# Weight sums of an up product made in device memory by adding transfers, and twelve of its tiles instead of eight in seven products

## The chip, the cores and the metric

The kernel runs on one core of one Trainium2 chip. The metric is device time in microseconds (us) of one run, and the number told is the median of several runs. Engines: PE (TensorE), DVE (VectorE), ACT (ScalarE), POOL (GpSimd), and SP (SyncE), which here only issues transfers.

## The reference

One layer of an encoder trunk on x of 1 x 512 x 1024, all in float32:

```
h  = rmsnorm(x, g_pre_mix)
q, k, v, g, u, sv, a_ret, a_sgu = split(h @ w_in)
y_ret = retention(q, k, v, g) @ w_ret_o           # 4 heads, chunks of 128
y_sgu = (gelu(u) * spatial(layernorm(gelu(sv)))) @ w_sgu_o
x1 = x + rmsnorm((sigmoid(a_ret) * y_ret + sigmoid(a_sgu) * y_sgu) @ w_out, g_post_mix)
h2 = rmsnorm(x1, g_pre_ffn)
a, b = split(conv3(h2 @ w_up))                    # 1024 -> 2 x 2816
y  = x1 + rmsnorm((gelu(a) * b) @ w_down, g_post_ffn)
```

The change is about `h2 @ w_up`.

## The kernel before, in words

**Precision.** Every matrix is split in a high and a low part (fp32r). ACT writes the high part (`copy`, L100), DVE subtracts it from the source to get the low part (`split`, L119), and PE makes three matmuls for each product of blocks: high by high, high by low, low by high.

**Weights.** All weights lie in one array `wall` in device memory, in blocks of 128 x 1024 (512 KB). A list of units gives the order in which they are used. `w_get` hands out a unit and loads ahead of it. A unit of the kind `blk` (`w_block`, L172) is a whole block: SP loads it into one of four `raw` buffers (L176), and its two parts go into two of nine slots. The four `raw` buffers are shared by all weights until the end.

**Seven products.** A pair of weight blocks against a pair of activation halves can be multiplied as a 2 x 2 matrix of blocks in seven products instead of eight (class `Pair`: `part1`, `part2`, `part3`; each product is 12 matmuls of 128 x 256, L926). That needs sums of the four weight quarters: T1 = B11 + B12, T3 = B12 + B22 (signs folded into the stored weights), T2 = T1 + B22, T4 = T2 + B21. `w_form` (L194) loads the two blocks (L198, L199), makes the sums in `raw` (L205, L206, L208, L211) and splits each of the seven forms, 512 columns wide, into one slot. In the gate stage POOL makes T2 and T4, in the up stage DVE makes all four. The matching sums of the activations (S1 to S4, `h2_forms`) are made once.

**The up product.** It has 22 tiles; tile i is 128 gate columns and 128 linear columns, in blocks UP0+2i and UP0+2i+1. Tiles 0 to 3, 20 and 21 are made whole: two `f_block` of 24 matmuls of 128 x 512 each (L300 to L302). Tiles 4 to 19 are taken as eight couples (`COUPLES`): the first tile by `Pair`, the second whole, its two `f_block` standing between the parts of the first. After each couple `tile_done` makes the convolution (L1247, L1250, L1254), gelu and product for both tiles. At some tiles `down_forms` makes sums of the results for the down product, whose low parts are partly made by adding transfers of POOL (`split_added`, L1273).

**What sets the order.** The program is recorded, and a scheduler then orders the instructions of each engine; `issue_after` ties an instruction behind another one, `keep_in_program_order` keeps those that carry it in the order of the program. On each engine's queue the order is then fixed: a transfer that an engine issues stands in its queue between its other instructions. Retention (heads 0 to 3, states `st`, keys `kz`, scores `sm`, decay `dec`, outputs normed with `rs`, `orstd`, `oshift`) and the SGU's `sv` product (L755, seven products too, with weights `sb` and `raw` that POOL adds to by L265 and L271) run up to about 200 us, the u, gate and mixing stages to 400, the output product and norms to 470, the up product to 669, the down product to 763.

Of the kernel before, what the change touches and what calls it, by code (L numbers as in the profile page):

```python
# [10 lines left out]
F32 = mybir.dt.float32  # L11
# [4 lines left out]
P = 128  # L16
D = 1024
S = 512
# [34 lines left out]
def tile_block(ctx: ExitStack, tc, xT, x, wall, par, cs, wsp, bsp, gpost, gffn, out):  # L53
# [30 lines left out]
    def tmp(n="tmp", shape=(P, S)):  # L84
        return sb.tile(list(shape), F32, tag="tmp", bufs=6, name=nm(n))
# [10 lines left out]
    def const(n, shape):  # L96
        return sb.tile(list(shape), F32, tag=n, bufs=1, name=n)

    def copy(o, i):
        return nc.scalar.activation(out=o, in_=i, func=AF.Copy)  # L100

    def two(t):
        return t.rearrange("p (n c) -> p n c", n=2)
# [24 lines left out]
    while i < NW:  # L128
        pair = [(f, i) for f in FORMS]
        if i == SV0:  # L130
            units += [(f, k) for f in ("s11", "sT1", "sT2") for k in range(2)]
            units += [(f, k) for k in range(2) for f in ("s22", "sT3")]
            units += [(f, k) for f in ("s21", "sT4") for k in range(2)]
            i = U0
        elif i == U0:
            us, gs = ([[(f, k + n * m) for f in FORMS] for n in range(KD // 2)] for k, m in ((U0, 2), (GATE0, 4)))
            ws = [("blk", GATE0 + 4 * (n // 2) + 2 + n % 2) for n in range(KD)]
            for what, n in MIDDLE:
                units += {"W": lambda: ws[n : n + 1], "U1": lambda: us[n][:4], "U2": lambda: us[n][4:],
                          "G1": lambda: gs[n][:4], "G2": lambda: gs[n][4:]}.get(what, list)()  # L140
            i = GATE0 + 2 * KD
        elif GATE0 <= i < GATE1:
            units += pair[:4] + [("blk", i + 2)] + pair[4:] + [("blk", i + 3)]
            i += 4
        elif i == UP0 + 2 * COUPLES[0][0]:
            for a, b in COUPLES:
                pair = [(f, UP0 + 2 * a) for f in FORMS]
                units += pair[:4] + [("blk", UP0 + 2 * b)] + pair[4:] + [("blk", UP0 + 2 * b + 1)]
            i = UP0 + 2 * COUPLES[-1][1] + 2
# [44 lines left out]
    def w_form(form, i):  # L194
# [19 lines left out]
        split(hi, lo, w_raw[form])  # L214
        return hi, lo

    def w_down(form, i):

        if form == "q":
            raw = w_raw["q"] = raw_tile()  # L220
            nc.sync.dma_start(raw, wall[i])
            raw = raw[:, : 3 * 256]
        else:
            b, raw = w_raw["q"], raw_tile()
            two = "p (n c) -> p n c"
# [50 lines left out]
        return hi, lo  # L276

    def w_unit(u):
        return w_block(u[1]) if u[0] == "blk" else (w_down if u[0] in "qt" else w_sv if u[0][0] == "s" else w_form)(*u)

    def w_size(u):
        return 2 if u[0] in ("blk", "q", "t") or u[0][0] == "s" else 1

    def w_get(look=LOOK):

# [623 lines left out]
    class Pair:  # L909
# [3 lines left out]
        def __init__(self, func, alloc, a=None, scale=None):  # L913
            self.func, self.t, self.scale = func, [alloc(), alloc()], scale
            self.h, self.l, self.forms = a or (xh, xl, forms)
            self.b = [ps() for _ in range(3)]
            self.two = in_turn if a is None else two

        def product(self, b, act, first, w=None):
            wh, wl = w or w_get()  # L920
            o = self.b[b][:, T0]
            for k in range(4):
                c = slice(k * P, (k + 1) * P)
                h_, l_ = act(k)
                for n, (w_, a_) in enumerate(((wh, h_), (wh, l_), (wl, h_))):
                    self.last = nc.tensor.matmul(  # L926
                        o, w_[:, c], a_, start=first and k == n == 0, stop=k == 3 and n == 2,
                        skip_group_check=True,
                    )
            pe_last[0] = self.last.ins  # L930
            return self.two(o)
# [27 lines left out]
        def part2(self):  # L959
            c0, c1 = self.t  # L960
            o = self.product(0, self.s("S3"), False)
            copy(two(c1[:, T1]), o)
            v.tensor_sub(two(c1[:, T1]), self.two(self.b[2][:, T0]), two(c1[:, T1]))
            self.w = w_get(), w_get()

        def part3(self):
            c0, c1 = self.t
# [340 lines left out]

    def tile_done(i, o):
        gated(*(conv(t, 2 * i + s_) for s_, t in enumerate(o)))  # L1310
        if i < COUPLES[-1][1]:
            if i in (7, 9, 11, 13, 17):
                down_forms(len(dforms))
        elif len(dforms) < EAGER:
            down_forms(len(dforms))

    def h2_forms(k):
# [9 lines left out]
            split(h_, l_, s_)  # L1327
            h2forms[n] += [(h_[:, t], l_[:, t]) for t in (T0, T1)]

    couples = dict(COUPLES)  # L1330
    i = 0
    while i < NF:
        if i in couples:
            p = Pair(None, lambda: tmp("c"), (h2h, h2l, h2forms))
            p.part1()
            o = [f_block(h2h, h2l, KD)]
            p.part2()
            o.append(f_block(h2h, h2l, KD, p.part3))
            tile_done(i, p.t)
            tile_done(i + 1, o)  # L1340
            i += 2
        else:
            o = []
            for e in (2 * i, 2 * i + 1):
                o.append(early_o[e] if e < EARLY else f_block(h2h, h2l, KD))
            tile_done(i, o)
            for k in {0: (0,), 1: (2,)}.get(i, ()):
                h2_forms(k)
            i += 1
# [234 lines left out]
    ], 1)  # L1584


def _up(a):

    for i, _ in COUPLES:
        b, c = a[2 * i].reshape(P, 2, S), a[2 * i + 1].reshape(P, 2, S)  # L1590
        a[2 * i : 2 * i + 2] = np.stack([
            np.concatenate([b[:, 0], c[:, 0]], -1), np.concatenate([c[:, 1], b[:, 1]], -1),
        ])
    return a
# [84 lines left out]
```

## Time and profile before

| | |
|---|---|
| runs | 782.95, 783.85, 784.19 us; median 783.85 |
| the profiled execution: span from first to last instruction | 782.6 us |
| median of the runs less that span | 1.25 us |
| instructions | 13472 |
| busy: PE, DVE, ACT, POOL | 774.5, 639.5, 485.2, 103.5 us |
| granted clock of TensorE | 0.997 |
| moved by transfers | 104.80 MB, mean 134 GB/s |

Times in the views are microseconds from the span's start. A group's row gives line, engine, operation, out<-in with shapes and count, then busy us and mean ns of one, then the engine's idle time ahead of it with its releasers. PE's matmuls overlap, so that the distance between two starts, not the duration of one, is what a matmul costs. The page names lines of the kernel before; in the changed kernel the same lines stand lower (`copy` at L105, the issue of the plain copies at L127, of the adding transfers at L119, the adding loads L265 and L271 at L319 and L325, `rsqrt` L459 and L462 at L515 and L518, `shift` L723 at L779).

### The profile page before, as it was taken

What the parts mean: (1) busy time and instruction counts of PE and PEld (TensorE: products, weight loads), DVE (VectorE), ACT (ScalarE), POOL (GpSimd) and SP (SyncE); (2) the same over time, 40 slices, a digit from 0 to 9 for tenths busy, and PEclk for the clock granted to TensorE, in tenths of its full rate; (3) what the DMA queues carried; (4) which work ended last, traced back from release to release, by engine and by line L of the source; (5) the groups of instructions that cost most, each with busy time, mean ns of one, the idle gap of its engine ahead of it and who ended that gap; (6) DMA issues with size and microseconds to landing.
All of it is one profiled execution on the core that took longest, in us unless ns stands there. A gap on an engine that the chain in (4) does not pass through costs nothing.

```text
span 782.6 us, 13472 instructions
## 1 busy us (share of the span) xinstructions
PE 774.5 (99%) x5139; PEld 720.7 (92%) x5139; DVE 639.5 (82%) x1093; ACT 485.2 (62%) x878; POOL 103.5 (13%) x132
## 2 busy tenths in 40 slices
PE   9999999999999999999999999999999999999996
PEld 8888998998999999999998998999999998999996
DVE  6567987789789988877765679989999889886987
ACT  7555568688466766644454686657777568644542
POOL 0040001130021102033211200001111012200001
PEclk9999999999999999999999999999999999999998
DMA  8783224453223233233459120435555375733344
GB/s 288 271 246 102 81 82 162 108 122 108 81 91 126 82 122 121 83 110 106 138 171 337 54 81 28 124 107 141 142 148 149 108 199 111 171 114 107 109 162 162
DMA packets 35889, 104.80 MB, mean 134 GB/s; under 512 B 4400, under 2 KB 6320, under 8 KB 35824
## 3 DMA queue, kind: packets, MB, share of 16 engines
q1 hardware_dynamic: 27936, 87.81, 34.0%
q0 software_dynamic: 7024, 14.95, 9.0%
q10 hardware_dynamic: 864, 1.18, 0.4%
q8 instruction: 40, 0.66, 0.4%
q14 instruction: 25, 0.20, 0.1%
HBM read 91.34 MB, written 4.19 MB: 122 GB/s over the span
## 4 chain that ended last, share of the span: by engine, by line
PE 92%; DVE 3%; DMA 3%; issue 1%; ACT 0%; POOLq 0%; DVEq 0%; POOL 0%; ACTq 0%
PE ps L926 24%; PE ps L300 12%; PE ps L302 12%; PE ps L301 12%; PE ps L1372 7%; PE ps L755 5%; PE ps L634 4%; PE ps L636 4%; PE ps L635 4%; DMA raw<-wall 3%; PE ps L1109 2%; PE ps L1108 2%; PE ps L1107 2%; DVE dl L119 1%; PE ps L997 1%
## 5 line engine op out<-in xcount | busy, mean ns | idle before, releaser
L119 DVE TENSOR_TENSOR wl<-raw,wh 128x1024 fp32r<-128x1024 f32 (+1 forms) x84 | 96.0, 1152 | 54.3 <-issue 19.1
L100 ACT ACTIVATE wf<-raw 128x512 fp32r<-128x512 f32 x140 | 85.6, 625 | 67.3 <-PE ps L301 19.4
L926 PE MATMUL ps<-sh,wf 128*128 128x256 f32 x640 | 117.4, 276 | 0.1
L119 DVE TENSOR_TENSOR wf<-raw,wf 128x512 fp32r<-128x512 f32 x140 | 107.0, 774 | 9.2 <-ACT wf L100 8.6
L926 PEld LDWEIGHTS ps<-sh,wf 128*128 128x128 f32 x640 | 101.9, 192 | 1.1 <-ACT sig L100 0.5
L100 ACT ACTIVATE wh<-raw 128x1024 fp32r<-128x1024 f32 (+2 forms) x88 | 84.8, 977 | 28.5 <-DMA raw<-wall 14.0
L300 PE MATMUL ps<-h2h,wh 128*128 128x512 f32 (+1 forms) x256 | 90.6, 354 | 0.0
L301 PE MATMUL ps<-h2l,wh 128*128 128x512 f32 (+1 forms) x256 | 90.4, 353 | 0.0
L302 PE MATMUL ps<-h2h,wl 128*128 128x512 f32 (+1 forms) x256 | 90.4, 353 | 0.0
L926 PE MATMUL ps<-sl,wf 128*128 128x256 f32 x320 | 88.0, 275 | 0.0
L926 PEld LDWEIGHTS ps<-sl,wf 128*128 128x128 f32 x320 | 61.4, 192 | 0.4
L1372 PE MATMUL ps<-dh,fh 128*128 128x256 f32 x216 | 59.6, 276 | 0.3 <-DVE yy L1409 0.3
L1372 PE MATMUL ps<-dl,fh 128*128 128x256 f32 x216 | 59.5, 275 | 0.0
L1372 PE MATMUL ps<-dh,fl 128*128 128x256 f32 x216 | 59.4, 275 | 0.0
L100 ACT ACTIVATE dh<-raw 128x768 fp32r<-128x768 f32 (+1 forms) x36 | 33.6, 950 | 33.8 <-DVE raw L231 15.2
L302 PEld LDWEIGHTS ps<-h2h,wl 128*128 128x128 f32 x256 | 48.6, 190 | 5.1
L301 PEld LDWEIGHTS ps<-h2l,wh 128*128 128x128 f32 x256 | 48.6, 190 | 4.5
L300 PEld LDWEIGHTS ps<-h2h,wh 128*128 128x128 f32 x256 | 48.6, 190 | 4.5
L926 PE MATMUL ps<-xh,wf 128*128 128x256 f32 x288 | 52.2, 275 | 0.0
L636 PE MATMUL ps<-wh,xl 128*128 128x512 f32 x128 | 48.5, 379 | 0.0
L635 PE MATMUL ps<-wl,xh 128*128 128x512 f32 x128 | 48.5, 379 | 0.0
L634 PE MATMUL ps<-wh,xh 128*128 128x512 f32 x128 | 48.5, 380 | 0.0
(343 smaller groups left out, 2171.6 us busy)
## 6 DMA issues: line engine op xcount, KB each, us to landing
raw<-wall SPq DMA_DIRECT2D x144, 512.0 KB, 3.7
x<-x SPq DMA_DIRECT2D x24, 256.0 KB, 6.0
fl<-gp POOLq DMA_DIRECT2D x12, 256.0 KB, 3.8
swap<-qkraw POOLq DMA_DIRECT2D x16, 128.0 KB, 4.8
x<-x POOLq DMA_DIRECT2D x8, 256.0 KB, 2.3
fl<-fs POOLq DMA_DIRECT2D x8, 256.0 KB, 4.3
xT<-xT SPq DMA_DIRECT2D x7, 256.0 KB, 5.0
xT<-xT POOLq DMA_DIRECT2D x4, 256.0 KB, 4.1
```

The lines of the kernel that those rows point to most:

```text
L100: return nc.scalar.activation(out=o, in_=i, func=AF.Copy)
L119: low[0] = nc.vector.tensor_sub(lo, src, as32(hi)).ins
L300: nc.tensor.matmul(o, ah, bh, start=start, stop=False, skip_group_check=skip)
L301: nc.tensor.matmul(o, ah, bl, start=False, stop=False, skip_group_check=skip)
L302: pe_last[0] = nc.tensor.matmul(o, al, bh, start=False, stop=stop, skip_group_check=skip).ins
L634: nc.tensor.matmul(acc[t], xh[k][:, c], turns(wh[:, f]), start=k == 0, stop=False)
L635: nc.tensor.matmul(acc[t], xh[k][:, c], turns(wl[:, f]), start=False, stop=False)
L636: part_end[0] = nc.tensor.matmul(acc[t], xl[k][:, c], turns(wh[:, f]), start=False, stop=k == KD - 1)
L755: nc.tensor.matmul(bank[t], a_[:, c], turns(w_[:, f]), start=first and k == i == 0, stop=last and k == 3 and i == 2, skip_group_check=True,)
L926: self.last = nc.tensor.matmul(o, w_[:, c], a_, start=first and k == n == 0, stop=k == 3 and n == 2, skip_group_check=True,)
L1107: nc.tensor.matmul(o, ah, turns(bh), start=k == 0, stop=False)
L1372: nc.tensor.matmul(o, a_[:, c], turns(w_[:, f]), start=j == t == i == 0, stop=j == DP - 1 and i == 2 and n not in (M2, M3, M4), skip_group ...
```

## The change

Tiles 4 to 19 become four groups of four (`GROUPS`). In each, the first three tiles a, b and c go through `Pair` and the fourth is whole, so that twelve of the 16 tiles are made in seven products rather than eight. The weight sums of these twelve tiles are made in device memory: `sum{i}_0` holds T1 and T2 side by side (512 KB), `sum{i}_1` T3 and `sum{i}_2` T4 (256 KB each). They are made during the earlier stages, at every 17th call of `copy` from the 36th on. Step n of 15 issues, on ACT right behind that copy, three plain transfers that fill tile n's sums, and on POOL four adding transfers: two for tile n-1, one for n-2, one for n-3. In all 36 issues on ACT and 48 on POOL. Counted in program order, these copies start at 75.6, 104.2, 134.1, 159.2, 169.9, 187.9, 211.8, 229.3, 249.7, 268.4, 288.5, 308.9, 329.4, 354.4 and 375.9 us in the profile of before.

In the up stage the forms are loaded and split 1024 wide, two forms at once (`u1` the block itself, `u2` T1 and T2, `u4` T4 and a quarter, two loads into one buffer), and T3 (`u3`) 512 wide. DVE's 32 sums of the up stage are gone. The rearranging of these weights on the host (`_up`) is gone too. `down_forms` are made at the same tiles as before.

```diff
-COUPLES = [(i, i + 1) for i in range(4, 20, 2)]
+GROUPS = range(4, 20, 4)
+SEVENS = [i + n for i in GROUPS for n in range(3)]
+SUMS_FROM, SUMS_EVERY = 36, 17
+FORMS_AT = (7, 9, 11, 13, 17, 19, 20, 21)
...
     def copy(o, i):
-        return nc.scalar.activation(out=o, in_=i, func=AF.Copy)
+        done = nc.scalar.activation(out=o, in_=i, func=AF.Copy)
+        copies[0] += 1
+        n, r = divmod(copies[0] - SUMS_FROM, SUMS_EVERY)
+        if n >= 0 == r:
+            sums_step(n, done.ins)
+        return done
...
+    def sums_step(n, after):
+
+        def add(o, i):
+            tc.keep_in_program_order(nc.gpsimd.dma_start(o, i, accum_op=ALU.add))
+
+        for m in range(n, n - 4, -1):
+            if 0 <= m < len(SEVENS):
+                (t12, t3, t4), i = sums[m], UP0 + 2 * SEVENS[m]
+                if m == n:
+                    with tc.issue_after(after):
+                        for o, src in ((t12, wall[i + 1]), (t3, wall[i + 1, :, :S]), (t4, wall[i, :, S:])):
+                            nc.scalar.dma_start(o, src)
+                elif m == n - 1:
+                    add(t12[:, :S], wall[i, :, :S])
+                    add(t3, wall[i + 1, :, S:])
+                elif m == n - 2:
+                    add(t12[:, S:], t12[:, :S])
+                else:
+                    add(t4, t12[:, S:])
...
+            for g in GROUPS:
+                a, b, c = ([(f, g + n) for f in ("u1", "u2", "u3", "u4")] for n in range(3))
+                w = [("blk", UP0 + 2 * (g + 3) + n) for n in range(2)]
+                units += a[:2] + b[:2] + a[2:3] + w[:1] + a[3:] + b[2:3] + c[:2] + b[3:] + c[2:3] + w[1:] + c[3:]
...
+    def w_up(form, i):
+
+        t12, t3, t4 = sums[SEVENS.index(i)]
+        raw, i = raw_tile(), UP0 + 2 * i
+        if form == "u3":
+            raw = raw[:, :S]
+            nc.sync.dma_start(raw, t3)
+            w = slot("wf", 0, 1088)
+            lo, hi = w[:, AT_64 : AT_64 + S], w[:, S + AT_192 : 2 * S + AT_192]
+        else:
+            if form == "u4":
+                nc.sync.dma_start(raw[:, :S], t4)
+                nc.sync.dma_start(raw[:, S:], wall[i + 1, :, S:])
+            else:
+                nc.sync.dma_start(raw, wall[i] if form == "u1" else t12)
+            hi, lo = slot("wf", AT_192), slot("wf", AT_64)
+        split(hi, lo, raw)
+        return hi, lo
...
+        if i in GROUPS:
+            a, b = seven(), seven(blk)
+            a.part2()
             o = [f_block(h2h, h2l, KD)]
-            p.part2()
-            o.append(f_block(h2h, h2l, KD, p.part3))
-            tile_done(i, p.t)
-            tile_done(i + 1, o)
-            i += 2
+            a.part3()
+            tile_done(i, a.t)
+            b.part2()
+            c = seven()
+            b.part3()
+            tile_done(i + 1, b.t)
+            c.part2()
+            o.append(f_block(h2h, h2l, KD, c.part3))
+            tile_done(i + 2, c.t)
+            tile_done(i + 3, o)
+            i += 4
```

Three places of the new order. First POOL near the third and fourth head's norms, before (`raw` and `sb` are adding loads for the `sv` product, `xT` a load of x):

```order
L856 DMA xT_329_1674<-xT 128x512
L856 DMA xT_331_1678<-xT 128x512
L459 TENSOR_SCALAR rs_318_1590<-mv_770 128x4
L462 TENSOR_TENSOR orstd_771<-rs_318_1590,nhalf_440 128x4
L723 TENSOR_TENSOR oshift_772<-oshift_772,orstd_771 128x4
```

And the same place of POOL in the changed kernel (`sum5_0` is the first sum tile of tile 5, and so on):

```order
L912 DMA xT_329_1724<-xT 128x512
L912 DMA xT_331_1728<-xT 128x512
L119 DMA sum6_0_69<-wall 128x512
L119 DMA sum6_1_70<-wall 128x512
L119 DMA sum5_0_66<-sum5_0_66 128x512
L119 DMA sum4_2_65<-sum4_0_63 128x512
L319 DMA raw_370_1883<-wall 128x1024
L515 TENSOR_SCALAR rs_318_1640<-mv_806 128x4
L518 TENSOR_TENSOR orstd_807<-rs_318_1640,nhalf_476 128x4
L779 TENSOR_TENSOR oshift_808<-oshift_808,orstd_807 128x4
```

Four adding transfers of the sums came in, and the first adding load of `raw` stands ahead of `rs`, `orstd` and `oshift`; before it stood right behind them.

Second ACT from the last head's `kz` to its `dec`, before (`sh` are high parts for the `sv` product):

```order
L100 ACTIVATE kz_1702<-kt_1700 128x512
L566 ACT_TABLE_LOAD
L566 ACTIVATE dec_1706<-near_503 128x128
L100 ACTIVATE sh_1687<-xs_1682 128x512
L566 ACTIVATE dec_1706<-near_503 128x128
L555 ACTIVATE dec_1706<-dd_501,lg 128x128
```

And in the changed kernel:

```order
L105 ACTIVATE kz_1752<-kt_1750 128x512
L127 DMA sum_0_72<-wall 16x8192
L105 ACTIVATE sh_1737<-xs_1732 128x512
L127 DMA sum_1_73<-wall 128x512
L105 ACTIVATE sh_1741<-xg_1726 128x512
L127 DMA sum_2_74<-wall 128x512
L622 ACT_TABLE_LOAD
L622 ACTIVATE dec_1763<-near_539 128x128 x2
L611 ACTIVATE dec_1763<-dd_537,lg 128x128 x2
```

The fourth step's three plain transfers stand between `kz` and `dec`, and a second `sh` moved ahead of `dec`.

Third SP's loads at the start of the up product's first group, in the changed kernel; before, each couple had two loads for its pair (L198, L199) and two for its whole tile (L176):

```order
L266 DMA raw_937_5458<-wall 128x1024
L266 DMA raw_941_5489<-sum4_0_63 128x1024
L266 DMA raw_948_5531<-wall 128x1024
L266 DMA raw_952_5562<-sum5_0_66 128x1024
L258 DMA raw_964_5609<-sum4_1_64 128x512
L211 DMA raw_966_5640<-wall 128x1024
L263 DMA raw_974_5676<-sum4_2_65 128x512
L264 DMA raw_974_5676<-wall 128x512
L258 DMA raw_977_5683<-sum5_1_67 128x512
```

The seven products of a tile take three and a half loads of 512 KB where they took two, and the sums come from device memory as loads.

More of the change, by code (lines that the diff above doesn't have):

```diff
@@ L97, in const @@
         return sb.tile(list(shape), F32, tag=n, bufs=1, name=n)
+    copies = [0]
     def copy(o, i):
-        return nc.scalar.activation(out=o, in_=i, func=AF.Copy)
+        done = nc.scalar.activation(out=o, in_=i, func=AF.Copy)
[4 more added lines that the diff above has]
+        return done
+    sums = [[
+        dp_.tile([P, w * S], F32, tag=f"sum{i}_{n}", name=f"sum{i}_{n}") for n, w in enumerate((2, 1, 1))
+    ] for i in SEVENS]
+    def sums_step(n, after):
[15 more added lines that the diff above has]
+                    add(t4, t12[:, S:])
     def two(t):
@@ L917, in __init__, with weight @@
             self.two = in_turn if a is None else two
+            self.ready, self.w = [], (None, None)
+        def weight(self):
+            if not self.ready:
+                hi, lo = w_get()
+                self.ready = [(hi[:, f], lo[:, f]) for f in HALVES[: hi.shape[-1] // S]]
+            return self.ready.pop(0)
         def product(self, b, act, first, w=None):
-            wh, wl = w or w_get()
+            wh, wl = w or self.weight()
             o = self.b[b][:, T0]
@@ L963, in part2 @@
             v.tensor_sub(two(c1[:, T1]), self.two(self.b[2][:, T0]), two(c1[:, T1]))
-            self.w = w_get(), w_get()
+            if self.h is xh:
+                self.w = self.weight(), self.weight()
         def part3(self):
@@ L1584, in _two @@
     ], 1)
[L1587 to L1594, printed above, removed]
 def _gates(a, w):
```

27 lines of the change are left out of this document (11 added, 16 removed).

## The prediction

> **What bounds the kernel now.** I read the page first, then the list of waits, the chain that ended last, the table by stretches, and last the groups and the timeline at the places that the change touches. TensorE (PE) is busy for 99% of the span. The list of what PE waited for (total us, times, longest) has two entries:
>
> ```profile
> PE 774.5 (99%) x5139; PEld 720.7 (92%) x5139; DVE 639.5 (82%) x1093; ACT 485.2 (62%) x878; POOL 103.5 (13%) x132
> PE ps L402 <- PEq L1669: 0.8, 1, 0.8
> PE ps L1372 <- DVE yy L1409: 0.3, 1, 0.3
> ```
>
> So from the first matmuls to the tail, time is lost only where PE does work, and a change gains what it takes from PE and loses what it makes PE wait. The table by stretches (PE, PEld, DVE, ACT, POOL busy, clock, DMA share, GB/s) says how near the others are:
>
> ```profile
> 0.00:100.00 100.00, 99.19 (x508) 87.46 (x509) 70.60 (x137) 59.17 (x102) 13.32 (x32) 1.00 0.59 196
> 100.00:200.00 100.00, 100.00 (x565) 90.03 (x565) 82.96 (x144) 76.16 (x135) 13.99 (x21) 1.00 0.42 117
> 200.00:300.00 100.00, 100.00 (x746) 95.55 (x745) 87.01 (x148) 64.62 (x111) 13.18 (x10) 1.00 0.32 101
> 300.00:400.00 100.00, 99.91 (x697) 93.87 (x697) 78.73 (x118) 52.32 (x88) 22.41 (x15) 1.00 0.38 125
> 490.28:648.20 157.92, 157.92 (x1058) 147.62 (x1057) 142.43 (x233) 107.39 (x193) 17.01 (x20) 1.00 0.50 139
> 647.00:684.00 37.00, 37.00 (x239) 34.29 (x238) 34.23 (x58) 28.49 (x47) 8.83 (x11) 1.00 0.62 143
> ```
>
> 490.28 to 648.20 is the eight couples of the up product: PE never stops there, DVE is busy for 90%. By the count of ACT's copies the sums are made between about 76 and 376 us, where the DMA share is 0.32 to 0.42.
>
> **The change part by part.** *PE in the up product.* The chain (start, us, what) shows one couple, and elsewhere seven and fourteen products in a row:
>
> ```profile
> 272.59 9.38 PE ps L926 x84
> 490.28 5.36 PE ps L926 x48
> 495.64 0.22 PE ps L300
> 500.82 1.34 PE ps L926 x12
> 502.16 0.22 PE ps L300
> 504.75 2.68 PE ps L926 x24
> 507.43 0.22 PE ps L300
> 510.02 5.36 PE ps L926 x48
> ```
>
> A couple takes 510.02 − 490.28 = 19.74 us. Its tile in seven products is 48 + 12 + 24 = 84 matmuls in 5.36 + 1.34 + 2.68 = 9.38 us, the length of the x84 row too. One half of its whole tile takes 500.82 − 495.64 = 5.18 us, the tile 10.36. A tile that goes over from whole to seven products saves 0.98 us. Among tiles 4 to 19 eight are in seven products now, and twelve will be: 4 × 0.98 = **3.92 us saved**. This is the only PE work that goes; the copies and subtractions of the four further tiles fall on ACT and DVE.
>
> *DVE and ACT there.* Groups of the up stretch on DVE, and of the whole run on ACT (busy us, mean ns):
>
> ```profile
> L119 DVE TENSOR_TENSOR wf<-raw,wf 128x512 fp32r<-128x512 f32 x54 | 36.5, 687 | 1.3 <-ACT wf L100 0.9
> L119 DVE TENSOR_TENSOR wl<-raw,wh 128x1024 fp32r<-128x1024 f32 x19 | 23.2, 1222 | 12.5 <-issue 10.4 <-ACT wh L100 2.1
> L1250 DVE SCALAR_TENSOR_TENSOR cv<-c,part,cv 128x511 f32<-128x511 f32 x14 | 10.5, 749 | 0.0
> L206 DVE TENSOR_TENSOR raw<-raw,raw 128x512 f32<-128x512 f32 x8 | 5.5, 690 | 0.2
> L211 DVE TENSOR_TENSOR raw<-raw,raw 128x512 f32<-128x512 f32 x8 | 5.5, 686 | 0.1
> L100 ACT ACTIVATE wf<-raw 128x512 fp32r<-128x512 f32 x140 | 85.6, 625 | 67.3 <-PE ps L301 19.4 <-issue 17.3 <-DMA raw<-wall 10.9
> L100 ACT ACTIVATE wh<-raw 128x1024 fp32r<-128x1024 f32 x72 | 76.0, 1058 | 24.8 <-DMA raw<-wall 10.4 <-PE ps L636 8.8 <-PE ps L301 4.0
> ```
>
> Two couples split 14 forms of 512 and 4 blocks of 1024: 14 × 0.687 + 4 × 1.222 = 14.5 us on DVE. A group of four splits 3 of 512 and 9 + 2 of 1024: 15.5. The eight sums of two couples, 0.69 each, leave DVE: −5.5. The third tile's four or so subtractions of 128x256 come with it (under 2 us). DVE goes from some 36 to some 33 in 38.5 us. ACT goes from 14 × 0.625 + 4 × 1.058 = 13.0 to 3 × 0.625 + 11 × 1.058 = 13.5, and a few copies more. Both stay below PE: **0**, and it stays 0 while weights arrive (second rival).
>
> *ACT's queue in the early stages.* Each of twelve steps puts three plain transfers on ACT. The nearest price is ACT's own first issue (ns, min/median/max); then follows the narrowest place that I found, where the last head's state st is made (timeline: start, us):
>
> ```profile
> L313 ACTq DMA_DIRECT2D raw<-wall x2: 420/435/450, 0.7 to 1.2; - x2
> 159.72 0.39 ACT L555 ACTIVATE dec<-dd,lg 128x128 f32<-128x128 f32 x1
> 160.45 1.28 DVE L675 SCALAR_TENSOR_TENSOR sm<-ps,dec 128x512 f32<-128x512 f32 x2
> 163.27 0.58 ACT L100 ACTIVATE st<-ps 128x512 fp32r<-128x512 f32 x1
> 165.29 0.68 DVE L119 TENSOR_TENSOR st<-ps,st 128x512 fp32r<-128x512 f32 x1
> 166.61 0.28 PE L300 MATMUL ps<-st,qx 128*128 128x256 f32 x1
> ```
>
> Three issues are 1.31 us. The fourth step's three stand between kz and dec in ACT's order, so dec ends at 161.4 rather than 160.1, and DVE's sm, next in its queue, waits; DVE then has no gap up to st. PE uses st 166.61 − 165.97 = 0.64 us after DVE has finished it. Ends: 0, if DVE's order changes or it makes the delay up, and 1.31 − 0.64 = 0.67. I take **+0.4**. ACT's other steps stand where its following results have more room, or ACT idle: for the eleven together 0 to 1.5, I take **+0.2**, since ACT is busy for 76 of 100 us at most.
>
> *POOL's queue.* 48 adding transfers are issued there. Rows of POOL's own adding transfers, POOL's gate sums, and the DVE split that follows the first:
>
> ```profile
> L1273 POOL DMA_DIRECT2D fl<-gp x20: 853/868/1545, 500.7 to 673.8; - x20
> L265 POOL DMA_DIRECT2D raw<-wall x2: 886/934/982, 148.6 to 150.7; - x2
> 217.04 1.34 POOL L208 TENSOR_TENSOR raw<-raw,raw 128x512 f32<-128x512 f32 x1
> 219.34 1.30 DVE L119 TENSOR_TENSOR wf<-raw,wf 128x512 fp32r<-128x512 f32 x2 [0.41 <-ACT wf L100]
> 220.90 18.76 PE ps L926 x168
> 244.65 1.66 POOL L211 TENSOR_TENSOR raw<-raw,raw 128x512 f32<-128x512 f32 x1 [3.83 <-DVE wf L119]
> ```
>
> 48 × 0.87 = 42 us on an engine that is busy for 13 to 22 in a hundred. A step is four issues, 3.5 us. One step stands ahead of the sum at 217.04, so that sum, its ACT copy and its split come up to 3.5 us late. The split now ends at 220.64; its product is the fifth of those from 220.90 on, of 18.76 / 14 = 1.34 us each, and begins at 226.3. Room 5.6 us: hidden. Other steps stand between two gate sums, in the gap of 3.83 us, or behind them: hidden. Near the end of the retention stage a step stands between two adding loads of sb: that load comes 3.5 us late. In order POOL also takes one adding load (L265) ahead of a head's rs and oshift; its source has to land first, or oshift waits with ACT behind it. For all of POOL 0 to 2; I take **0** by choice, as no wait of PE here shows that it is near either load.
>
> *Into the down product.* From 647 to 684 DVE is busy for 34.23 of 37 us, and PE waits 0.3 us for yy further on. The last group ends, as the last couple did, with one tile in seven products and one whole tile, and DVE comes there with less behind it. Between −0.3 and +1.0; taken **0**.
>
> Sum: −3.92 + 0.4 + 0.2 = **−3.3 us**. The profiled span of 782.6 becomes 779.3. The median of the runs, 783.85, lies 1.25 above that span, which I take as constant: **780.5**.
>
> **The rivals.** *1. The small queue delays are not small.* Four ACT steps, and the later POOL load, meet the retention stage, where ACT's timeline has hardly a gap. For: st's room of 0.64 us. Against: PE is fed far ahead elsewhere. If four steps each cost the 0.67 of st, 2.7 instead of 0.6: 782.6.
>
> *2. The up product's loads become the bound (slower).* A group loads 12.5 units of 512 KB where two couples load 8; four raw buffers carry them. Groups and queues of DMA:
>
> ```profile
> raw<-wall SPq DMA_DIRECT2D x144, 512.0 KB, 3.7
> DMA to landing us min/median/max: 3.4/3.7/6.8
> q1 hardware_dynamic: 27936, 87.81, 34.0%
> q0 software_dynamic: 7024, 14.95, 9.0%
> ```
>
> That is 2.36 MB more in 38.5 us, 61 GB/s on 139; the share would go from 0.50 to 0.72. In the run of eleven products at a group's border PE uses up a buffer each 2 × 1.34 us, so a buffer must come round in 10.7 us. With 3.7 for landing, 1.06 and 1.22 for the split, and 2.5 in the queues (one item of 1.06 on ACT, two of 0.74 on DVE) it takes 8.5; it decides against the change from a landing of 5.9 us on. At the slowest landing, 6.8, it is 11.6, 0.9 too long, 0.22 a buffer: 6 buffers × 4 groups × 0.22 = 5.4 us, 785.9. Against: between 0 and 100 us the share is 0.59 at 196 GB/s and PE works 99.19 of 100. The Trainium skill (DMA: Bandwidth & Descriptors, Latency and other measured facts) gives an HBM access 0.2 us on average and 2 us under high load; as an estimate by that page a landing would be 5.5, just short of the point, and the time unchanged. No row here shows the latency alone.
>
> *3. The sums' transfers slow the loads of the middle stages.* At q1's rate (87.81 MB in 34.0% of 782.6 us) the 12.6 MB copied fill 38 us of all engines, at q0's the 12.6 MB added 59: 97 us within 300, and the shares of 0.32 to 0.42 become 0.64 to 0.74. The Trainium skill (the same page, Issuing engines are not separate DMA queues) says so of transfers from any engine: they interleave on the same 16 DMA engines, and only issue time is saved. If a gate load lands at 6.8 instead of 3.7, its sum is 3.1 late, and with a step of 3.5 ahead of it 6.6, 1.0 over the room of 5.6. If three of the eight gate pairs meet that: +3.0, 783.5. Against: the same row of 0 to 100 us.
>
> *4. More than 3.9 is gained*, as DVE's freed time also removes the wait for yy and no queue delay shows: 779.6. The sums are used some 100 us after the last one, so PE cannot wait for them.
>
> **How the numbers follow.** Forecast, 779.6 to 782.3 with the fourth case: 0.65. First rival 0.13, second 0.13, third 0.09. A measurement of this kernel tells about 0.2%, 1.6 us. Faster (below 782.3): 0.65 and some of the first and third, 0.70. Same: 0.14. Slower (above 785.4): most of the second, a little of the others, 0.16. The range goes from 779.2, just below the full gain, to the second rival's 786.0.
>
> **What would show it right or wrong.** Right: four groups of 38.5 us in the chain, without a wait for raw, wf or ps; PE's list of waits under 1 us; L205 to L211 gone from DVE after 490 us. Rival 1: PE waits at st or sv near 160 to 176. Rival 2: PE waits for wf in the up product, and raw lands there in 6 us or more. Rival 3: waits in the gate stage behind POOL's sums. A total of PE waits over 3 us makes the prediction wrong, and so does a group over 39.

## The result, and the profile after

The changed kernel takes 811.1 us (median of 5 runs, 807.07 to 811.67) against 783.61 for the kernel before: ratio 1.034, interval 1.0322 to 1.0358. It is slower by 27.5 us, where 780.5 was forecast. The profiled execution took 809.88 us, its span 807.9.

The page's first line and the six longest rows of what PE waited for (total us, times, longest) after the change:

```profile
PE 776.3 (96%) x5283; PEld 723.5 (90%) x5283; DVE 631.3 (78%) x1057; ACT 492.5 (61%) x878; POOL 144.3 (18%) x180
PE ps L989 <- ACT sig L105: 10.0, 6, 2.8
PE ps L989 <- ACT u L105: 6.3, 3, 2.8
PE ps L989 <- ACT c L105: 2.2, 3, 0.9
PE ps L357 <- DVE st L153: 1.5, 1, 1.5
PE ps L1459 <- DVE wl L153: 1.2, 1, 1.2
PE ps L1443 <- DVE c L1485: 1.0, 1, 1.0
```

PE waited 1.1 us before and waits some 25 now. The largest two entries are copies out of PSUM that ACT makes in the u and gate products; `wf`, the weights of these products, is not on the list. The stretches (PE, PEld, DVE, ACT, POOL busy, clock, DMA share, GB/s) show where:

```profile
0.00:100.00 100.00, 98.88 (x510) 86.89 (x511) 70.56 (x137) 58.01 (x103) 15.37 (x34) 1.00 0.64 206
100.00:200.00 100.00, 97.68 (x550) 87.26 (x549) 77.61 (x137) 73.50 (x129) 26.46 (x36) 1.00 0.79 208
200.00:300.00 100.00, 91.28 (x653) 86.25 (x652) 77.65 (x130) 54.38 (x98) 28.39 (x29) 0.98 0.70 181
300.00:400.00 100.00, 92.42 (x649) 86.44 (x648) 78.99 (x122) 53.76 (x90) 30.11 (x25) 1.00 0.56 150
513.02:690.74 177.72, 175.57 (x1298) 166.98 (x1298) 151.47 (x231) 129.73 (x214) 19.20 (x22) 1.00 0.64 181
```

The last row covers the four groups and the two whole tiles behind them. PE idles for 16 us between 200 and 400, where the DMA share has gone from 0.32 and 0.38 to 0.70 and 0.56. Loads of 512 KB between 200 and 350 us land in 6.2 us, before in 3.5 (DMA view of that stretch: first the sums' transfers and the loads after the change, then the loads before it):

```profile
raw<-wall SPq DMA_DIRECT2D x26, 512.0 KB, 6.2
sum<-wall POOLq DMA_DIRECT2D x14, 256.0 KB, 7.0
sum<-sum POOLq DMA_DIRECT2D x14, 256.0 KB, 9.8
sum<-wall ACTq DMA_DIRECT2D x6, 512.0 KB, 4.9
```

```profile
raw<-wall SPq DMA_DIRECT2D x29, 512.0 KB, 3.5
```

And ACT's own waits for these loads in the same stretch, before and after:

```profile
ACT wf L100 <- DMA raw<-wall: 9.5, 8, 1.9
```

```profile
ACT wf L105 <- DMA raw<-wall: 30.9, 12, 6.4
ACT wh L105 <- DMA raw<-wall: 7.5, 2, 4.7
```

One such place in ACT's timeline after the change; PE's next matmul starts 3.07 us after the one at 240.47:

```profile
239.94 1.06 ACT L105 ACTIVATE wh<-raw 128x1024 fp32r<-128x1024 f32 x1 [4.65 <-DMA raw<-wall]
239.96 1.79 ACTq L127 DMA_DIRECT2D sum<-wall  x3
241.79 0.38 ACT L105 ACTIVATE sig<-ps 128x256 f32<-128x256 f32 x1 [0.79 <-issue]
```

ACT stands 4.65 us at the split of a block whose first matmul starts only at 249.19. The three issues of a step come next, and only then the copy `sig`, for which PE waits: in these rows ACT works its queue in order, so the late load delays what stands behind the split that waits for it.

PE waits nine times for `sig` and `u`, 16.3 us together. Before four of these waits, 8.6 us, ACT had just waited for a load. Before the first, at 229 us and 1.7 us long, it had waited for a sum that POOL makes, late behind POOL's issues of a step:

```profile
225.32 1.16 ACT L105 ACTIVATE wf<-raw 128x512 fp32r<-128x512 f32 x2 [1.94 <-POOL raw L243]
```

Before the other four, at 261, 306, 340 and 350 us, ACT was at work or waited for DVE.

Lengths of four stages on PE, in us from the first matmul of one to the first of the next, from the profiles of all kernels below. By the lines of the kernel before, the stages begin with the first matmul of L634, of L926, of L1107 and of L1372; the last ends with the last matmul of L1388.

| kernel | retention and sv | u, gate, mixing | output and up product | down product |
|---|---|---|---|---|
| before | 162.1 | 192.8 | 265.7 | 106.6 |
| after | 165.5 | 212.4 | 264.8 | 110.2 |
| e1 sums only | 166.1 | 212.3 | 265.7 | 106.2 |
| e2 sums, narrow | 166.6 | 194.7 | 266.6 | 105.7 |
| e3 plain transfers only | 163.3 | 195.7 | 266.0 | 105.7 |
| e4 no sums | 162.1 | 193.1 | 264.9 | 108.8 |
| e5 sums late | 162.1 | 201.7 | 289.0 | 108.2 |
| e6 forms moved | 162.1 | 193.0 | 264.9 | 108.9 |
| e7 sums only, five buffers | 162.8 | 209.0 | 268.7 | 105.7 |
| e8 before, five buffers | 163.9 | 193.8 | 268.7 | 106.8 |
| e9 forms by DVE | 162.1 | 192.9 | 265.1 | 111.9 |
| e10 sums of four tiles | 165.7 | 193.2 | 266.0 | 105.7 |
| e11 c by DVE | 162.1 | 193.1 | 273.0 | 108.9 |
| e12 sums at half pace | 162.2 | 201.9 | 266.1 | 106.2 |
| e13 halves of 512 | 162.1 | 193.1 | 264.6 | 107.9 |
| e14 less ahead | 162.1 | 192.9 | 265.1 | 108.1 |

After less before: +3.4, +19.6, -0.9 and +3.6, in sum 25.7 us. The span grew by 25.3, since the first of these matmuls came 0.3 us earlier. The up product gains 0.9 where 3.9 was forecast.

### The profile page after: what moved, and what is told of

Its sections match the earlier page's. It is cut to its first block, busy times and chain, and to the rows that moved or that the text cites. A ratio compares the mean times of both kernels' runs of the same rounds, so it can differ in the third digit from the quotient of the medians.

```text
span 807.9 us, 13972 instructions
## 1 busy us (share of the span) xinstructions
PE 776.3 (96%) x5283; PEld 723.5 (90%) x5283; DVE 631.3 (78%) x1057; ACT 492.5 (61%) x878; POOL 144.3 (18%) x180
## 3 DMA queue, kind: packets, MB, share of 16 engines
q0 software_dynamic: 13936, 27.53, 18.5%
## 4 chain that ended last, share of the span: by engine, by line
PE 64%; DVE 14%; DMA 10%; ACT 6%; issue 4%; POOL 1%; POOLq 0%; ACTq 0%; DVEq 0%; SPq 0%
PE ps L989 16%; DMA raw<-wall 10%; PE ps L357 8%; PE ps L358 8%; PE ps L356 8%; PE ps L1443 7%; PE ps L690 3%; PE ps L692 3%; PE ps L691 3%; DVE wf L153 3%; PE ps L811 2%; PE ps L1171 2%; PE ps L1172 2%; PE ps L1173 2%; DVE wl L153 1%
## 5 line engine op out<-in xcount | busy, mean ns | idle before, releaser
L989 PE MATMUL ps<-sh,wf 128*128 128x256 f32 x768 | 142.6, 278 | 16.1 <-ACT sig L105 7.6
L105 ACT ACTIVATE wf<-raw 128x512 fp32r<-128x512 f32 (+1 forms) x132 | 96.0, 743 | 92.7 <-DMA raw<-wall 35.5
L153 DVE TENSOR_TENSOR wf<-raw,wf 128x512 fp32r<-128x512 f32 (+1 forms) x132 | 122.5, 941 | 31.9 <-ACT wf L105 30.8
L989 PEld LDWEIGHTS ps<-sh,wf 128*128 128x128 f32 x768 | 123.0, 193 | 19.2 <-ACT sig L105 9.0
L989 PE MATMUL ps<-sl,wf 128*128 128x256 f32 x384 | 106.2, 277 | 0.0
L356 PE MATMUL ps<-h2h,wh 128*128 128x512 f32 (+1 forms) x192 | 66.3, 345 | 0.0
L357 PE MATMUL ps<-h2l,wh 128*128 128x512 f32 (+1 forms) x192 | 66.1, 344 | 0.0
L358 PE MATMUL ps<-h2h,wl 128*128 128x512 f32 (+1 forms) x192 | 66.1, 344 | 0.0
L1443 PE MATMUL ps<-dh,fh 128*128 128x256 f32 x216 | 59.8, 277 | 1.7 <-DVE c L1485 1.0
L1443 PE MATMUL ps<-dl,fh 128*128 128x256 f32 x216 | 59.5, 275 | 0.0
L1443 PE MATMUL ps<-dh,fl 128*128 128x256 f32 x216 | 59.4, 275 | 0.0
L989 PE MATMUL ps<-h2h,wf 128*128 128x256 f32 x288 | 52.3, 275 | 0.0
L989 PEld LDWEIGHTS ps<-xh,wf 128*128 128x128 f32 x288 | 45.9, 193 | 2.8 <-ACT sig L105 2.5
L989 PEld LDWEIGHTS ps<-h2h,wf 128*128 128x128 f32 x288 | 45.7, 192 | 0.3
```

Of the source, the lines that this page charges most:

```text
L105: done = nc.scalar.activation(out=o, in_=i, func=AF.Copy)
L153: low[0] = nc.vector.tensor_sub(lo, src, as32(hi)).ins
L356: nc.tensor.matmul(o, ah, bh, start=start, stop=False, skip_group_check=skip)
L357: nc.tensor.matmul(o, ah, bl, start=False, stop=False, skip_group_check=skip)
L358: pe_last[0] = nc.tensor.matmul(o, al, bh, start=False, stop=stop, skip_group_check=skip).ins
L989: self.last = nc.tensor.matmul(o, w_[:, c], a_, start=first and k == n == 0, stop=k == 3 and n == 2, skip_group_check=True,)
```

## The experiments

**e1, the sums alone.** The kernel before, with `sums_step` and its call in `copy`, and nothing that reads the sums:

```diff
     def copy(o, i):
-        return nc.scalar.activation(out=o, in_=i, func=AF.Copy)
+        done = nc.scalar.activation(out=o, in_=i, func=AF.Copy)
...
+            sums_step(n, done.ins)
```

> The kernel before, with the 36 plain and 48 adding transfers of the changed kernel, and nothing that uses them; the up product is as before. Theory A (the bytes of the sums' transfers delay the weight loads of the middle stages; ACT's split waits for a late load, and the copies out of PSUM queued behind it make PE wait) and theory B (the time that the issues take on ACT's and POOL's queues delays the gate sums and the copies) both expect the loss of the early and middle stages, about +22 us: 806. Theory C (the new up product costs the time) expects 784.

Measured: 809.14 us against 783.44, ratio 1.0326 (1.029 to 1.0361). The transfers alone cost 25.7 us, in the same two stages as in the changed kernel. Theory C falls as the main cause.

**e2, a quarter of the bytes.** On e1, with N = 128, and so for each of the transfers:

```diff
-        add(t12[:, :S], wall[i, :, :S])
+        add(t12[:, :N], wall[i, :, :N])
```

> As the kernel with the transfers alone, with the same number of transfers, rows and issues, but only 128 of each 512 columns moved, a quarter of the bytes (the sums are not complete and nothing uses them). Theory A expects most of the loss to go: below 790, with loads landing in about 4 us in the gate stage. Theory B expects 800 or more, since the issues stay.

Measured: 790.38, ratio 1.0087 (1.0066 to 1.0107). That is 0.4 us above what theory A asked for, far below theory B. The gate stage's loss falls from 19.5 to 1.9 us, with loads that land in 3.7 us, though the issues keep POOL as long as in e1 (1020 and 1444 ns in the middle, against 960 and 1441); so there it is the bytes. The loss in the retention stage does not fall at all (4.5 after 4.0): there it is not the bytes.

**e3, plain transfers only.**

```diff
-                elif m == n - 1:
-                    add(t12[:, :S], wall[i, :, :S])
...
```

> The kernel before, with the 36 plain transfers from ACT alone; no adding transfers. In the changed kernel the plain ones took 5.0% of the DMA engines' time, the adding ones 9.5%. Theory A expects about a third of the loss: 789 to 793. Theory B, if the issues on ACT are what costs, expects 800; if those on POOL, 785.

Measured: 787.56, ratio 1.0051 (1.003 to 1.0071), a sixth of the loss: less than the 789 to 793 of theory A, and between the two values of theory B. The page's queues, first of e1 with everything, then of e3:

```profile
q0 software_dynamic: 13936, 27.53, 18.8%
q10 hardware_dynamic: 4704, 13.77, 4.9%
```

```profile
q0 software_dynamic: 7024, 14.95, 9.1%
q10 hardware_dynamic: 4704, 13.77, 5.3%
```

The 12.6 MB added take twice the engine time of the 12.6 MB copied (18.8 - 9.1 against about 5 hundredths of the span), and cost five times as much on top of them, 21.6 us against 4.1. No run had the adding transfers alone.

**e4, the new up product without the sums' transfers.**

```diff
-        t12, t3, t4 = sums[SEVENS.index(i)]
         raw, i = raw_tile(), UP0 + 2 * i
+        t12, t3, t4 = wall[i + 1], wall[i + 1, :, :S], wall[i, :, S:]
```

> The changed kernel without the sums' transfers: the up product loads blocks of the stored weights where it loaded sums, so its sums are left out and the values differ, while loads, splits and products stay the same in number and size. Theories A and B expect the early and middle stages as before, and the up and down stages as in the changed kernel: -0.9 and +3.6, so about 786.5. If the late stages lose only through what the transfers left behind, 780.

Measured: 785.54, ratio 1.0027 (1.0017 to 1.0037): still slower than before, by 2.1 us. The early stages are as before, the up product gains the same 0.9, and the down product loses 2.2. So 3.0 of the 3.9 us are missing in the up product whatever the transfers do. The chain at the first of its three waits:

```profile
534.25 4.30 DMA raw<-wall
...
538.63 1.07 ACT wf L103
539.70 0.51 ACT fl L1305
540.21 0.61 ACT fh L103 x2
540.83 0.61 ACT fl L1305 x2
541.44 0.30 ACT fh L103
541.74 0.28 ACT c L103
...
542.06 1.60 PE ps L958 x12
```

The copy `c` stands in ACT's queue behind a wide split that waits for its load (0.35 us of ACT's time), and behind the forms for the down product; the product that adds onto its bank waits for it. At the other two places ACT waits for nothing: it works without a gap from 564.80 and from 603.77 us until the copy ends at 572.80 and 612.43, on forms, convolutions and splits. The end of the first of these stretches:

```profile
570.59 1.43 ACT L1280 ACTIVATE cv<-ps,part 128x512 f32<-128x512 f32 x2
571.91 0.62 ACT L103 ACTIVATE wf<-raw 128x512 fp32r<-128x512 f32 x1
572.43 0.37 ACT L103 ACTIVATE c<-ps 128x256 f32<-128x256 f32 x1
```

PE's list has 2.2 us for the three waits; the starts of the matmuls on both sides of them are 1.23, 1.16 and 0.74 us apart instead of 0.11, so they cost 2.8 of the 3.0 us.

**e5, the sums after the gate stage.**

```diff
-SUMS_FROM, SUMS_EVERY = 36, 17
+SUMS_FROM, SUMS_EVERY = 240, 10
```

> The changed kernel with its 15 steps of sums after the gate stage: from copy 240 on, every 10 copies, about 330 to 560 us, so that retention and the gate stage run without them and a tile's sums are still done before its use. Theory A expects the 22.7 us of those two stages back, and a smaller loss in the mixing stage and the up product, whose loads are fetched further ahead: 785 to 790. If any stage under this traffic loses as the gate stage did (theory A without the point on lead), 800 or more. Theory B expects the issue time to cost where POOL has its adding loads of the up product: 790 to 795.

Measured: 818.83, ratio 1.0447 (1.0425 to 1.0469), slower than the changed kernel. The milder expectation is missed, and the 800 or more of theory A without the point on lead came. Retention and the gate stage up to 330 us are as before, but seven of the steps lie within 100 us, and the DMA engines are full:

```profile
350.00:400.00 50.00, 45.45 (x285) 42.01 (x284) 32.49 (x44) 18.95 (x32) 20.76 (x19) 0.97 0.83 215
400.00:450.00 50.00, 39.26 (x199) 34.22 (x197) 22.16 (x32) 19.08 (x35) 12.68 (x16) 0.96 0.99 304
500.00:550.00 50.00, 46.85 (x315) 44.36 (x313) 35.90 (x51) 28.01 (x46) 11.82 (x14) 0.93 1.01 294
PE ps L1241 <- DVE xn L1226: 8.9, 1, 8.9
```

One wait of 8.9 us is in the norm behind the output product, whose rows of x are loaded there. A part of the loss is PE's own pace: the granted clock was 0.50 from 446 to 456, 538 to 545 and 589 to 593 us, where PE was busy for 15.0 us. Half of that, by estimate 7.5 us, is in the 23.3 that the output and up product lose.

**e6, the forms elsewhere.** On e4:

```diff
-FORMS_AT = (7, 9, 11, 13, 17, 19, 20, 21)
+FORMS_AT = (5, 8, 9, 13, 17, 19, 20, 21)
```

> The changed kernel without the sums' transfers (blocks of weights loaded in the sums' place, so the values differ), with the forms of the down product made at tiles 5, 8, 9, 13, 17 instead of 7, 9, 11, 13, 17. Theory D: the 3 us that the up product falls short of its 3.9 are PE's three waits for the copies of c, which stand in ACT's queue behind the forms made at a group's end; then these go, the up product takes 3.0 us less, and the time is 782 to 783.5 against 785.5. If the waits come from the three products' interleaving itself, the time stays at 785.5.

Measured: 785.54, ratio 1.0024 (1.0014 to 1.0033), the time of e4. Theory D falls: PE has again three waits for c, 1.9 us, at other places.

**e7 and e8, five raw buffers, with the sums and without.**

```diff
-        return sb.tile([P, 1024], F32, tag="raw", bufs=4, name=nm("raw"))
+        return sb.tile([P, 1024], F32, tag="raw", bufs=5, name=nm("raw"))
...
-        return sb.tile([P, 1088], F32R, tag="w4", bufs=9, name=nm(n))[:, at : at + w]
+        return sb.tile([P, 1088], F32R, tag="w4", bufs=8, name=nm(n))[:, at : at + w]
```

> The kernel before with the sums' transfers and nothing that uses them, with five raw buffers instead of four (and eight weight slots instead of nine, for the room). Theory A on lead: a load that starts one buffer earlier hides most of the 2.5 us by which landings grew, so less than half of the 25.7 us is left, beside its own control: below 797. If the loss is not in lead (theory B), 805 or more.

> The control for the kernel with five raw buffers: the kernel before with five raw buffers and eight weight slots, no sums. All theories expect 783 to 788, since PE did not wait before; it says what the missing slot costs.

Measured: 801.88 (1.0232, 1.0211 to 1.0252) and 789.31 (1.0071, 1.0051 to 1.0091). The number expected by theory A, 797, is missed, and so is the 783 to 788 expected of the control. Beside its control the loss is 12.6 us instead of 25.7, just under half, but the control itself loses 5.7, with 1.8 of it in the retention stage, where the sums cost time too. The gate stage tells more: 15.2 us beside the control instead of 19.5, with loads that still land in 6.0 us. There one more buffer (and one slot less) hides less than a quarter.

**e9, the low parts of the forms by DVE.** On e4:

```diff
-        apart = split_added if j < EAGER else split
+        apart = split
```

> The changed kernel without the sums' transfers (blocks of weights in the sums' place, so the values differ), with all low parts of the down product's forms made by DVE rather than by a negated copy on ACT and an adding transfer of POOL. Theory E: PE's waits for c in the up product come from ACT, whose queue holds 1024-wide splits that wait for a load, and the forms' copies, ahead of c; without 28 copies on ACT they shrink, and the up product takes 1.5 to 3 us less, 782.5 to 784 against 785.5, unless DVE becomes late into the down product. If ACT is not the cause, 785.5 or more, with the same three waits.

Measured: 788.63, ratio 1.0064 (1.0047 to 1.008). Theory E falls too: the waits for c are 2.5 us, and DVE is late into the down product, which takes 111.9.

**e10, the sums of four tiles.** On e1:

```diff
-SEVENS = [i + n for i in range(4, 20, 4) for n in range(3)]
+SEVENS = [4, 5, 6, 8]
```

> The kernel before with the sums' transfers of four tiles only (12 plain, 16 adding), all but the last two steps in the retention and sv stages, and nothing that uses them. The kernel with all twelve tiles lost about 3.5 us there and 19.5 in the gate stage. Theory F: the loss of the first part is one of order and issue on ACT's and POOL's queues, since a quarter of the bytes lost as much; it stays, the gate stage's goes: 786.5 to 788. If the transfers' bytes cost the same per tile everywhere (25.7 / 12 = 2.1 us), 792.

Measured: 787.84, ratio 1.0064 (1.0041 to 1.0088), as theory F expects. The retention stage loses 3.6 us, the gate stage 0.4. Two places of that loss are seen in the changed kernel. The first is POOL's timeline, before and after:

```profile
147.77 0.24 POOL L723 TENSOR_TENSOR oshift<-oshift,orstd 128x4 f32<-128x4 f32 x1
```

```profile
146.32 0.91 POOL L319 DMA_DIRECT2D raw<-wall  x1 [4.78 <-DVE oshift L774]
147.30 0.45 POOL L515 TENSOR_SCALAR rs<-mv 128x4 f32<-128x4 f32 x1
147.84 1.36 POOL L518 TENSOR_TENSOR orstd<-rs,nhalf 128x4 f32<-128x4 f32 x1
149.27 0.29 POOL L779 TENSOR_TENSOR oshift<-oshift,orstd 128x4 f32<-128x4 f32 x1
```

The adding load that now stands ahead of `rs` begins only at 146.32, and `oshift` ends at 149.56, 1.5 us later than before. ACT waits for it with the outputs, and `kz` behind them starts 1.5 us later too. The second place is ACT's way from `kz` to `dec`:

```profile
159.28 0.63 ACT L105 ACTIVATE sh<-xs 128x512 fp32r<-128x512 f32 x1 [1.09 <-DVE xs L497]
160.74 0.64 ACT L105 ACTIVATE sh<-xg 128x512 fp32r<-128x512 f32 x1 [0.83 <-DVE xg L499]
```

Both `sh` wait for DVE and now stand ahead of `dec`. From the start of `kz` to the end of `dec` it takes 6.2 us, before 4.1. The step's issues run beside these copies (0.50 us from 159.28, 0.51 from 160.76) and do not hold ACT up. e3, which has only ACT's transfers, shows the same 6.2 us with `oshift` in time (147.50) and loses 1.2 us in the stage; e12 below, which has no step at this place, shows 4.1 and loses 0.1.

**e11, c by DVE.** On e4:

```diff
+            move = copy if self.h is xh else v.tensor_copy
...
-            copy(two(c0[:, T0]), o)
+            move(two(c0[:, T0]), o)
...
-            self.copied = copy(two(c1[:, T0]), o).ins
+            self.copied = move(two(c1[:, T0]), o).ins
```

> The changed kernel without the sums' transfers (blocks of weights in the sums' place, so the values differ), with the two first copies of c of every tile in seven products of the up product made by DVE rather than ACT. Theory G: these copies come late because ACT's queue holds wide splits ahead of them that wait for weight slots and loads; on DVE, which has lost the sums, they are in time, PE's three waits go and the up product takes 2 to 3 us less: 782.5 to 784 against 785.5. If DVE's queue has the same splits ahead of them, the waits stay, now for DVE, and the time is 785 to 788.

Measured: 790.96, ratio 1.0092 (1.0075 to 1.0109). Theory G is missed as a cure, and the time lies above both ranges: PE now waits 6.2 us for the same copies on DVE. DVE's queue holds splits ahead of them too, and it is fuller: DVE is busy for 134 us from 490 to 650, ACT in e4 for 116. At 495.10, 578.07 and 599.51 us the copy stands directly behind the convolution of the tile before (L1288).

**e12, the sums at half pace.** On e1:

```diff
-SUMS_FROM, SUMS_EVERY = 36, 17
+SUMS_FROM, SUMS_EVERY = 36, 34
```

> The kernel before with the sums' transfers at half the pace (a step each 34 copies, so that they go on to the end of the kernel; the last adding transfer falls away) and nothing that uses them. If the loss goes by bytes alone, the steps that fall in the gate stage are half as many, and what is spread over the other stages costs as much each: about 809 as before. Theory A with a threshold (a late load costs only beyond the lead of its buffer) expects clearly less: 790 to 798.

Measured: 793.25, ratio 1.0124 (1.0104 to 1.0144). That lies in the range of theory A with a threshold, far below 809. In the gate stage five steps start instead of nine, with 35 of the 49 transfers that e1 issues there and 73% of their bytes; it loses 9.1 us instead of 19.5, which is 46%. So the loss falls faster than the bytes, as it would if a load's lead had to be used up first; two runs do not show such a threshold. The steps that fall in the other stages cost nearly nothing (+0.1, +0.4, -0.4). So the same transfers are dear in the gate stage and cheap in the up product at the same pace.

**e13 and e14, narrow splits, and weights fetched less far ahead.** On e4:

```diff
+            split(hi[:, :S], lo[:, :S], raw[:, :S])
+            hi_, lo_, raw_ = hi[:, S:], lo[:, S:], raw[:, S:]
+            split(hi_, lo_, raw_)
+            return hi, lo
```

```diff
-                hi, lo = w_get()
+                hi, lo = w_get(LOOK if self.h is xh else 2)
```

> The changed kernel without the sums' transfers (blocks of weights in the sums' place, so the values differ), with the wide forms split in two halves of 512 columns each, in the same buffers and slots. Theory I: the 1024-wide splits block ACT's and DVE's queues for too long ahead of the copies of c; halves let the copies through, PE's waits in the up product fall by half or more and the time comes to 783 to 784.5. If width is not the cause, the waits stay at 2 us or grow with the added instructions: 785.5 to 788.

> The changed kernel without the sums' transfers (blocks of weights in the sums' place, so the values differ), with weights of the twelve tiles fetched two slots' worth ahead rather than as far as nine slots hold. Theory J: the copies of c stand behind splits that were fetched so far ahead that they wait for weight slots; with fewer ahead, the waits of PE for c go, and the time comes to 783 to 784.5. If the splits ahead are not the cause, 785.5; if loads then come too late, PE waits for wf and the time is 788 or more.

Measured: 784.72 (1.0019, 1.001 to 1.0028) and 785.35 (1.0029, 1.0016 to 1.0041). Neither removes the waits:

```profile
PE ps L962 <- ACT c L103: 2.0, 3, 0.8
```

These are e13's. Its time is 0.8 us under e4's, with intervals that overlap; the wait for `wl` in the down product is shorter there. Theory I falls as a single cause. e14 limits the calls in `Pair` to six slots (four for a form of 512 columns), the unit in hand included, and leaves those in `f_block` as they were, so that theory J is tested in part: PE has three waits for c again, 2.1 us.

## Why the prediction was wrong

**PE in the up product, 3.92 saved.** The products did go: the 0.9 us gained and the 2.8 lost in waits make 3.7 of the 3.9. But the step behind it, ACT and DVE "0", failed. I compared busy times with PE's and did not ask what stands ahead of each copy. Three waits of PE for copies of c take 2.8 us back, in e4 too, where no sums are made. At one place a split that waits for its load and the forms stand ahead; at the other two ACT has worked without a gap for 8 us on forms, convolutions and splits. That is what the trace shows; which single one of them to move is open. Moving the forms, taking their low parts off ACT, moving the copies, halving the splits and fetching less far ahead each left 1.9 us of waits or more. No run moved the convolutions, behind which the copies stand in e11 too.

**ACT's queue, +0.4 and +0.2.** The place, `st`, was right; the mechanism and the size were not. Retention and sv lose 3.4 us. I priced the three issues, at 435 ns each. They took 598 in the middle, but at this place they run beside ACT's copies. What makes `dec` late on ACT is the order that the step brought: two `sh` that wait for DVE stand ahead of it, for 2.1 us. e3, with ACT's transfers alone, loses 1.2 us. And the term for POOL, "0 to 2, taken 0 by choice", is the larger part, 2.8 us from e3 to e1: the adding load ahead of `oshift` did make it wait, as the prediction named it. e2 loses as much in this stage with a quarter of the bytes. This is the first rival, with a price of 2.7 us; it came beside the third.

**POOL's gate sums, "hidden".** One was not: PE waits 1.7 us at 229 us behind it, and 1.3 us at the same place in e2. That is the small part of the stage; e2 keeps POOL's issues and loses 1.9 us there.

**The third rival** was the right one, with a chance of 0.09 and a price of 3.0. Its mechanism was half right. The share rose to 0.79, 0.70 and 0.56 (0.64 to 0.74 expected) and loads landed in 6.2 us (6.8 assumed). The step that failed is the price: I set a load that is 3.1 us late against the room of 5.6 us that PE has until it uses those weights. In that stage PE never waited for weights. ACT waited for the load, at the head of a queue that also holds the copies out of PSUM, and for these PE has hardly any room. The row for that was there: ACT already waited 9.5 us for raw from 200 to 350 us in the kernel before. It waited 38.4 us after, 11.4 in e2, 27.2 in e12 and 15.3 in e7, where the stage lost 19.6, 1.9, 9.1 and (beside its control) 15.2 us: the loss follows these waits only loosely. That the bytes cause it is shown by e2; that it reaches PE through ACT's order is read in the rows, and no run changed that order in the gate stage. The row used against it, 0.59 of DMA share from 0 to 100 us with PE at 99.19, proved nothing for another stage. e12 and e5 show how much the stage and the pace decide: about 2 us a step in the gate stage, almost nothing in the up product at half pace, and 23.3 us in the output and up product when the steps are close.

The rule that I named there (the Trainium skill, DMA: Bandwidth & Descriptors, Issuing engines are not separate DMA queues) is borne out: transfers issued by ACT and POOL took SP's loads from 3.5 to 6.2 us.

**Into the down product, 0.** It lost 3.6 us in the changed kernel and 2.2 in e4, above the end of +1.0. In e4 PE waits 1.5 us for the low part `wl` of the first whole block; DVE's order has a sum ahead of it whose load it awaits for 3.82 us:

```profile
PE ps L1428 <- DVE wl L122: 1.5, 1, 1.5
685.47 0.69 DVE L249 TENSOR_TENSOR raw<-raw 128x512 f32<-128x512 f32 x1 [3.82 <-DMA raw<-wall]
686.08 0.68 DVE L122 TENSOR_TENSOR fl<-gp,fh 128x512 fp32r<-128x512 f32 x1
686.68 1.22 DVE L122 TENSOR_TENSOR wl<-raw,wh 128x1024 fp32r<-128x1024 f32 x1
```

The changed kernel's list has 1.2 us for `wl` and 1.0 more for `c` (L1443), which DVE makes behind a sum whose load it awaits for 2.16 us. The rest is open.

**The second rival** did not come: raw lands in 3.9 us in the up product, and PE does not wait for `wf` there. Nor did the fourth: the wait for `yy` is still 0.3 us.

## What to carry to other kernels

When transfers are added beside a stage, look at which engine's queue waits for that stage's loads, and at what stands behind the wait in the same queue, not at how long the loaded data has until it is used. A stretch with as high a DMA share and no loss is no evidence for another stage; a run with the transfers alone, unused, prices them in one go. And sums moved from a vector engine into memory are paid for in transfers: those of 12 tiles cost 25.7 us here, for 3.9 us of products at best. Where a new instruction enters a queue, look also at which others change places with it: two copies that came to stand ahead of `dec` made it 2.1 us late, the issues beside them by nothing that shows.

## What the runs showed of the hardware

Adding 12.6 MB in device memory took 18.5% of 807.9 us less 9.0% of 782.6, 79 us of all 16 engines. Copying as much from ACT took 5.0% less the 0.4% of before, 37 us. The issue of an adding transfer kept POOL for 960 ns (source in `wall`) and 1437 ns (source in the sums), against the 868 taken from before.

A wait of PE can cost more than its length. Behind the one that ends at 243.54 us in the changed kernel the granted clock (the column after POOL's) is half for 3.4 us:

```profile
243.60:246.70 3.10, 3.10 (x15) 3.10 (x16) 1.40 (x3) 1.44 (x3) 0.00 (x0) 0.50 0.95 249
246.90:250.00 3.10, 3.10 (x26) 3.02 (x26) 0.96 (x2) 0.90 (x2) 0.00 (x0) 1.00 0.46 185
```

15 matmuls start there, 26 in as long a time after it: by estimate 1.7 of the gate stage's 19.6 us. Behind another wait as long, which ends at 337.32 us, the clock stays at 1.00. What decides it is not shown.
